# A two-layer streaming encoder step: the first layer's FFN-out as 2x2 blocks in seven products

## The chip, the cores and the metric

The kernel runs on one core of a Trainium2 chip. The metric is the device time of one execution in microseconds, the median of several runs. A core has TensorE (PE in the profile, with its weight loads as PEld), VectorE (DVE), ScalarE (ACT), GpSimd (POOL) and SyncE (SP), which here issues nearly all DMAs. Matmuls take fp32 operands split into two parts of type fp32r, a high and a low one, so a product of two matrices is three passes: high by high, high by low, low by high.

## The reference

One step over 1088 columns (1024 prompt frames and 64 frames of a running stream) with a model width of 1024. Layer 0 has an SSD mixer, layer 1 a chunk-band attention, each followed by a SwiGLU FFN with 2816 hidden rows:

```python
def swiglu(u, w_in, w_out):
    g, up = jnp.split(u @ w_in, 2, axis=-1)
    return (jax.nn.silu(g) * up) @ w_out

# per layer, for the prompt and the sample alike
xp = xp + rmsnorm(mp, nw[1])                      # mp: mixer or attention
xp = xp + rmsnorm(swiglu(rmsnorm(xp, nw[2]), ffn_w_in[layer], ffn_w_out[layer]), nw[3])

# layer 1 starts from the residual stream after layer 0
kv = rmsnorm(x, kv_norm_w) @ w_kv                 # shared K and V
q  = rmsnorm(xp, nw[0]) @ attn_w_q[i]
```

The change touches `... @ w_out` of layer 0, where the sums of weights for both layers are made, and the first weights of `w_kv` and `attn_w_q`.

## The kernel before, in words

Activations lie with features on partitions (tiles of 128 rows) and frames on columns. The work runs in the order SSD mixer, layer 0's FFN-in, layer 0's FFN-out, K/V/Q projections and attention, output projection, layer 1's FFN-in, layer 1's FFN-out.

*The order of the work.* PE's instructions are issued in the order in which the program writes them. A small planner, `Stream` (L94), keeps a simulated time `st.t` that grows by columns/2360 us for each matmul. Side tasks (generators: norm chains, loaders, ends of slices) yield a delay and a condition, and `pump` lets those go on whose time has come, so their few matmuls fall among the main ones at that place in PE's queue. The other engines' instructions are ordered by priority; `tc.high_priority(n)` moves a group ahead. Constants such as `ER_W`, `EQ_W` are such delays. SP issues its DMAs in one queue. `Weights` (L236) holds a list of planned weight tiles: `load` issues the DMA into one of two `raw` buffers (or one lent for the stage), then ACT copies the high part and VectorE subtracts for the low part (`part`, L362 to L372); three such pairs fit. A weight with `kscale` goes through `scaled` (L375): eight ACT and eight VectorE instructions, one per 128 columns, with a norm weight multiplied in.

*FFN-in* of both layers is in seven products (P1 to P7) of 2x2 blocks: rows of the weight by two, frames by two. `BO, BN` split the frames into block 0 (512) and block 1 (576), each of two halves, so matmuls have 256 or 288 columns; the four halves are the quarters q0 to q3 of `QS`. `run_pair` (L1469) does a pair of gate and up tiles, in the order of `RUN[layer]`; its evictions run on ACT and VectorE (`add`, `times`, L1483 to L1535).

*Layer 0's FFN-out* is plain: each of three slices of frames (384, 384, 320), each of 8 blocks of 128 rows, 22 blocks of the hidden dimension, three passes (L1901 to L1903). The hidden activations go to DRAM (`hd`) in FFN-in (class `Plain`, `row`) and come back split by `loader` (L1710). After a slice, `end` (L1792) makes the post-norm, adds the residual from `x1d`, writes `x2d`, splits the result into the operands `u[s]` of attention, and forms the next norm's factor in `rba[s]`; while later slices run, only the last slice's `end` remains beside attention's first units (one unit is a weight tile on a slice: 8 x 3 matmuls).

*Layer 1's FFN-out* is in seven products (`wino`, L1546; matmuls L1596 to L1598). Class `Hidden` forms four sums of blocks of the hidden activation on VectorE in FFN-in (`form`, L1395; the operations are L1408) and stores seven operands in `hop`. The four sums of blocks of the weight (`wt`) are formed in *layer 0's* FFN-in by `Plain.chunk` (L1337, operations on L1347), from loads into the five stage buffers `sg`. Such operations wait in a list `late`; one is issued after each product of `run_pair`. `wino` runs the products in `PHASES`: P1, P6, P2, P7, P5 on both blocks, then P4 on block 0, P4 on 1, P3 on 1, P3 on 0; it keeps P3's weights in SBUF from the first to the second. Quarter q0 is complete after P4 on block 0, q2 after P4 on 1, q3 after P3 on 1, q1 after P3 on 0. `end7` (L1764) ends a quarter.

*Attention's start* (L2221): `wv, wk, wq` of the first pair of heads on slice 0, then on slice 1, then a second `wk` on both, then slice 2. Each evicted unit needs `rba[s]`.

Of the kernel before, what the change touches and what calls it, by code (L numbers as in the profile page):

```python
# [49 lines left out]
ES = 0.5, 0.5, 0.0  # L50
OS = 1.9, 1.4
EP_W, ER_W, EQ_W = (9.4, 9.4, 5.0), (8.9, 8.9, 4.5), (11.0, 11.0, 11.0)
# [5 lines left out]
LDP, ENP, ATP = 1500, (0, 0, 1500), 1000  # L58
# [11 lines left out]
LAHEAD, LGAP = 2, (1.5, 0.5)  # L70
# [3 lines left out]
RUN = (  # L74
    [(t, (0, 1)) for t in range(NB0, FT)] + [(t, (1,)) for t in range(NB0)],
    [(5, (0, 1)), (4, (1,))] + [(t, (0, 1)) for t in range(6, FT)] + [(t, (1,)) for t in range(4)],
)
# [329 lines left out]
PHASES = [(p_, (0, 1)) for p_ in (P1, P6, P2, P7, P5)] + [(P4, (0,)), (P4, (1,)), (P3, (1,)), (P3, (0,))]  # L407
# [4 lines left out]
def hybrid_kernel(  # L412
# [39 lines left out]
    hop = dr.tile([P, 7, KH, T // 2], F32, name="hop")  # L452
    wt = dr.tile([P, 4, 4, FH], F32, name="wt")
# [61 lines left out]
    def add_sq(ssum, src, n, first, eng=None):  # L515
        if first:
            A.activation(ssum[:, :n], src, AF.Square)
        else:
            q = nsb.tile([P, 384], F32, tag="sq", bufs=2, name="sq")
            A.activation(q[:, :n], src, AF.Square)  # L520
            (eng or G).tensor_tensor(ssum[:, :n], ssum[:, :n], q[:, :n], op=ALU.add)  # L521
# [32 lines left out]
    def bcast(dg, a, n, rb=None):  # L554
# [4 lines left out]
        if rb is None:  # L559
            rb = nsb.tile([P, 384], F32, tag="rb", bufs=1, name="rb")  # L560
        A.copy(rb[:, :n], bp[:, :n])
# [703 lines left out]
    def phys(layer, t_):  # L1265
        return t_ // 2 + KH * (t_ % 2) if layer else t_
# [6 lines left out]
    def ffn_plan(layer):  # L1273
        w1, w2 = w_f1[layer], w_f2[layer]
        W.plan(*[dict(src=[w1[i]]) for t_ in range(NB0) for i in (phys(layer, t_), FT + phys(layer, t_))])
        for i, (t_, bs) in enumerate(RUN[layer]):
            it = dict(src=[w1[phys(layer, t_)], w1[FT + phys(layer, t_)]])
# [3 lines left out]
        if not layer:  # L1281
            for s in range(NSL):
                for m in range(KD):
                    for k0, nk in KCH:
                        W.plan(dict(src=[w2[m][:, k0 * P:(k0 + nk) * P]], n=nk * P))
            return
        for p_, _ in PHASES[:-1]:
            for j in range(4):
                for i, (k0, nk) in enumerate(KIT):
                    if p_ in (P1, P2, P3):  # L1290
                        v = half(w2[j + 4 * (p_ == P3)], p_ != P1, k0, nk)
                    else:
                        v = wt[:, j, {P6: WT2, P7: WT3, P5: WT1, P4: WT4}[p_], k0 * P:(k0 + nk) * P]
                    it = dict(src=[v], n=nk * P, lend=1)
                    if p_ == P3 and 2 * j + i >= HLB:
                        it["keep"] = R
                    W.plan(it)

    KCH = ((0, 8), (8, 8), (16, 6))

    class Plain:

        def __init__(self):
            self.late = []

        def order(self, bs):
            pass

        def first(self, b, t_):
            return False  # L1310

        def out(self, b, t_, row, other):
            return other

        def row(self, b, t_, row, v):
            n = v.shape[1]
            nc.sync.dma_start(hd[:, t_, BO[b] + row * n:BO[b] + (row + 1) * n], v)

        def sums(self, b, t_, c, u_):
            pass  # L1320

        def side(self, i):


            if i == 0:
                self.todo, self.got = [(j, k0, nk) for j in range(4) for k0, nk in WCH], []
                self.load()
            if self.todo:
                self.late += [lambda gate, i=i: self.chunk(i, gate) for i in range(4)]

        def load(self):
            w2, (j, k0, nk) = w_f2[1], self.todo[0]
            self.got = [stage[0]()[:, :nk * P] for _ in range(4)]
            for t_, m, h in zip(self.got, (j + 4, j + 4, j, j), (1, 0, 0, 1)):
# [1062 lines left out]
```

## Time and profile before

| | |
|---|---|
| median of 3 runs | 3046.65 us (3046.03 to 3050.11) |
| the profiled execution | 3048.59 us, span of its instructions 3046.8 us |
| mean granted clock of TensorE | 0.988 |
| PE, PEld, DVE, ACT, POOL busy | 97%, 95%, 72%, 48%, 22% of the span |
| DMA | 385.70 MB, 127 GB/s on the mean |
| layer 0: FFN-in; FFN-out | 941 to 1361 us; 1361 to 1635 us of the span |
| layer 1: FFN-in; FFN-out | 2367 to 2791 us; 2791 to 3032 us |

A line of a group reads: line of the kernel, engine, operation, output tile <- input tiles, shape, count | busy us, mean ns of one | idle time of the engine just before them, and what ended it. Matmuls are pipelined, so the mean of one is longer than the distance between two starts; cadences are read from the timeline. In tables by stretch, the columns after the length are the busy us (and instructions) of PE, PEld, DVE, ACT and POOL, then the granted clock, the share of the DMA engines and GB/s.

### The profile page before, as it was taken

What the parts mean: (1) busy time and instruction counts of PE and PEld (TensorE: products, weight loads), DVE (VectorE), ACT (ScalarE), POOL (GpSimd) and SP (SyncE); (2) the same over time, 40 slices, a digit from 0 to 9 for tenths busy, and PEclk for the clock granted to TensorE, in tenths of its full rate; (3) what the DMA queues carried; (4) which work ended last, traced back from release to release, by engine and by line L of the source; (5) the groups of instructions that cost most, each with busy time, mean ns of one, the idle gap of its engine ahead of it and who ended that gap; (6) DMA issues with size and microseconds to landing.
All of it is one profiled execution on the core that took longest, in us unless ns stands there. A gap on an engine that the chain in (4) does not pass through costs nothing. (4 is left out here: it accounts for less than half of the span.)

```text
span 3046.8 us, 58392 instructions
## 1 busy us (share of the span) xinstructions
PE 2949.8 (97%) x22017; PEld 2883.7 (95%) x22017; DVE 2193.8 (72%) x4906; ACT 1475.2 (48%) x2834; POOL 660.6 (22%) x852
## 2 busy tenths in 40 slices
PE   9999999999999999999999999999898999999999
PEld 8899999999999999999999898999898899999998
DVE  8988888885878665684666777767668765558567
ACT  6665656554444333354454655555544433335452
POOL 1334444421342221111231000000053212211011
PEclk9999999999999999999999999999999999999999
DMA  3433333335543544555664222212344333236665
GB/s 119 114 92 103 96 100 96 99 115 164 155 133 118 156 132 152 157 163 171 203 192 135 75 66 81 62 63 73 112 148 132 101 112 119 80 104 201 190 190 190
DMA packets 244843, 385.70 MB, mean 127 GB/s; under 512 B 25584, under 2 KB 197168, under 8 KB 244560
## 3 DMA queue, kind: packets, MB, share of 16 engines
q1 hardware_dynamic: 244496, 381.89, 40.6%
q8 instruction: 173, 2.83, 0.4%
q14 instruction: 110, 0.90, 0.1%
q0 software_dynamic: 64, 0.07, 0.0%
HBM read 293.54 MB, written 83.86 MB: 124 GB/s over the span
## 5 line engine op out<-in xcount | busy, mean ns | idle before, releaser
L495 PE MATMUL mm<-r,hl 128*128 128x384 f32 (+2 forms) x1632 | 548.4, 336 | 7.1 <-ACT r L2210 6.2
L497 PE MATMUL mm<-r,hl 128*128 128x384 f32 (+2 forms) x1632 | 530.2, 325 | 3.5 <-DVE hl L383 2.8
L496 PE MATMUL mm<-r,hl 128*128 128x384 f32 (+2 forms) x1632 | 529.4, 324 | 0.7 <-DVE r L2211 0.7
L371 DVE TENSOR_TENSOR hl<-raw,hl 128x1024 fp32r<-128x1024 f32 (+1 forms) x245 | 287.2, 1174 | 204.4 <-ACT hl L370 203.0
L1501 PE MATMUL px<-r,hl 128*128 128x288 f32 (+1 forms) x1192 | 350.5, 294 | 0.4 <-DVE r L1192 0.3
L370 ACT CAST hl<-raw 128x1024 fp32r<-128x1024 f32 (+1 forms) x245 | 240.8, 984 | 189.8 <-PE po L1903 48.2
L495 PEld LDWEIGHTS mm<-r,hl 128*128 128x128 f32 x1632 | 311.0, 191 | 8.9 <-ACT r L2210 6.4
L1500 PE MATMUL px<-r,hl 128*128 128x288 f32 x1056 | 311.9, 295 | 4.6 <-ACT p L1512 2.6
L497 PEld LDWEIGHTS mm<-r,hl 128*128 128x128 f32 x1632 | 310.2, 190 | 5.0 <-DVE hl L383 4.0
L496 PEld LDWEIGHTS mm<-r,hl 128*128 128x128 f32 x1632 | 311.2, 191 | 1.3 <-DVE r L2211 1.0
L1502 PE MATMUL px<-r,hl 128*128 128x288 f32 x1056 | 311.3, 295 | 0.0
L521 POOL TENSOR_TENSOR ssum<-ssum,sq 128x256 f32<-128x256 f32 (+3 forms) x146 | 157.8, 1083 | 510.0 <-ACT sq L520 494.6
L1500 PE MATMUL px<-rx,hl 128*128 128x256 f32 x816 | 229.7, 281 | 9.9 <-ACT p L1512 9.9
L1502 PE MATMUL px<-rx,hl 128*128 128x256 f32 x816 | 228.5, 280 | 0.0
L1501 PEld LDWEIGHTS px<-r,hl 128*128 128x128 f32 x1192 | 224.3, 188 | 0.9 <-DVE r L1192 0.8
L1500 PEld LDWEIGHTS px<-r,hl 128*128 128x128 f32 x1056 | 199.0, 188 | 6.0 <-ACT p L1512 3.5
L1502 PEld LDWEIGHTS px<-r,hl 128*128 128x128 f32 x1056 | 198.8, 188 | 0.0
L1501 PE MATMUL px<-rx,hl 128*128 128x256 f32 x680 | 190.6, 280 | 0.0
L1489 DVE TENSOR_TENSOR c<-px,u 128x256 f32<-128x256 f32 (+1 forms) x78 | 34.5, 442 | 198.1 <-ACT u L1512 198.1
L1512 ACT COPY u<-px 128x288 f32<-128x288 f32 (+1 forms) x156 | 60.4, 388 | 224.3 <-PE px L1502 224.1
L1500 PEld LDWEIGHTS px<-rx,hl 128*128 128x128 f32 x816 | 155.0, 190 | 10.6 <-ACT p L1512 10.6
L1502 PEld LDWEIGHTS px<-rx,hl 128*128 128x128 f32 x816 | 155.1, 190 | 0.0
(421 smaller groups left out, 8589.8 us busy)
## 6 DMA issues: line engine op xcount, KB each, us to landing
raw<-in_w_f_dram SPq DMA_DIRECT2D x156, 512.0 KB, 3.8
raw<-in_w_in_dram SPq DMA_DIRECT2D x40, 512.0 KB, 3.7
raw<-in_w_so_dram SPq DMA_DIRECT2D x32, 512.0 KB, 3.9
raw<-in_w_f_dram SPq DMA_DIRECT2D x33, 384.0 KB, 3.3
dm<-acd SPq DMA_DIRECT2D x64, 192.0 KB, 3.7
sg<-hop SPq DMA_DIRECT2D x77, 144.0 KB, 3.1
sg<-hop SPq DMA_DIRECT2D x83, 128.0 KB, 3.2
sg<-in_w_f_dram SPq DMA_DIRECT2D x48, 192.0 KB, 3.5
```

What stands on the lines that cost most here:

```text
L370: self.nc.scalar.copy(h, v)
L371: (eng or self.eng or self.nc.vector).tensor_tensor(lo, v, h, op=ALU.subtract)
L495: PE.matmul(ps[:, :n], h_, xh, start=(first and i == 0), stop=False)
L496: PE.matmul(ps[:, :n], h_, xl, start=False, stop=False)
L497: PE.matmul(ps[:, :n], l_, xh, start=False, stop=(last and i == nk - 1))
L521: (eng or G).tensor_tensor(ssum[:, :n], ssum[:, :n], q[:, :n], op=ALU.add)
L1489: V.tensor_tensor(x[d], x[bank][:, :n], x[y or d], op=ALU.add)
L1500: PE.matmul(ps, wh, ah[:, k, :], start=(k == 0 and not on), stop=False, skip_group_check=on)
L1501: PE.matmul(ps, wh, al[:, k, :], start=False, stop=False, skip_group_check=on)
L1502: PE.matmul(ps, wl, ah[:, k, :], start=False, stop=(k == 3), skip_group_check=on)
L1512: A.copy(hid.gate, ps)
```

## The change

Layer 0 uses `Hidden` and `wino` as layer 1 does. `Plain`, `loader`, `end_load` and `end` go. Both layers use layer 1's order of pairs (`RUN`). Each layer has its own `hop` and `wt` in DRAM and forms its weight sums in its own FFN-in, between pairs 2 and 16 (`side`). In layer 0 the last phases are P4 on 0, P4 on 1, P3 on 0, P3 on 1, and P3's weights are loaded for each block. `EndU` ends the quarters of layer 0: attention's slices are cut differently from quarters (`PARTS`), so quarter 1 is split in two parts and quarter 2 gives its last 32 columns to slice 2 in a later step; residuals come through the stage buffers, those of q3 ahead into two `r` buffers. `prescale` multiplies six attention weights by their norm weights during FFN-out and stores them in `wsc` in DRAM; eight planned weights then need no scaling. At attention's start a unit is evicted after the next unit's matmuls.

```diff
-EP_W, ER_W, EQ_W = (9.4, 9.4, 5.0), (8.9, 8.9, 4.5), (11.0, 11.0, 11.0)
+PARTS = [(0, 0, 0, 256)], [(0, 256, 0, 128), (1, 0, 128, 256)], [(1, 128, 0, 256), (2, 0, 256, 288)], [(2, 32, 0, 288)]
+EP_W, ER_W, EQ_W = (3.0, 3.0, 3.0), (5.5, 7.0, 5.5, 4.5), (18.0, 2.5, 14.0, 22.0)
...
+PHASES = [
+    [(p_, (0, 1)) for p_ in (P1, P6, P2, P7, P5)] + end_
+    for end_ in ([(P4, (0,)), (P4, (1,)), (P3, (0,)), (P3, (1,))], [(P4, (0,)), (P4, (1,)), (P3, (1,)), (P3, (0,))])
+]
...
         def order(self, bs):
...
-            for o in g:
-                self.late += o
+            self.late = [f for o in g for f in o] + self.late
...
         def side(self, i):
...
+            if i in (1, 7):
+                self.load()
+            elif self.todo and (i == 2 or 8 <= i < FT - 5):
+                self.late += [lambda gate, i=i: self.chunk(i, gate) for i in range(4)]
+                if i % 2 == 0:
+                    self.late += [lambda gate: None] * 3
+                    self.late += [lambda gate, i=i: self.chunk(i, gate) for i in range(4)]
...
     def wino(...):
...
-                    if p_ != P3:
+                    if p_ != P3 or not layer:
                         W.put()
...
+                if not layer:
+                    if p_ == P4 and j == 0:
+                        W.pri = HIP
+                    if (p_, bs) == phases[-1] and j == 0:
+                        st.spawn(end.ahead())
...
+            def prescale():
+                for i, (v, c) in enumerate(FIRST):
+                    for c0, c1 in ((0, 3), (3, 6), (6, 8)):
+                        t = stage[0]()[:, :(c1 - c0) * P]
+                        nc.sync.dma_start(t, v[:, c0 * P:c1 * P])
+                        yield 0, PS_W
+                        t3 = t.rearrange("p (k m) -> p k m", m=P)
+                        V.tensor_tensor(t3, t3, c[:, c0:c1].unsqueeze(2).to_broadcast([P, c1 - c0, P]), op=ALU.mult)
+                        nc.sync.dma_start(wsc[:, i, c0 * P:c1 * P], t)
+                        yield 0, PS_G
...
+            class EndU:
...
+                def split(self, q, y, m, s, c, c0, c1):
+                    ym = y[m // 4][:, m % 4, c0:c1]
+                    uh, ul = (v[:, c:c + c1 - c0] for v in u[s][m])
+                    with tc.high_priority(ENP[q]):
+                        A.copy(uh, ym)
+                        V.tensor_tensor(ul, ym, uh, op=ALU.subtract)
...
+                def __call__(self, q, y, ss, more):
...
+                    yield from rb_steps(ss, n, out, ER_W[q], more=more)
+                    tot = [ssum_start(n) for _ in range(1 + last)]
+                    def tail(m):
...
+                            self.split(q, y, m, *part)
+                        with tc.high_priority(ENP[q]):
+                            add_sq(tot[m % len(tot)], y[m // 4][:, m % 4, :], n, m < len(tot), G if q < 2 or m % 2 else V, None if last else xs[m])
+                    for m in range(KD):
+                        ym = y[m // 4][:, m % 4, :]
+                        with tc.high_priority(ENP[q]):
+                            V.scalar_tensor_tensor(ym, ym, col(cpost2 + m), out[0], op0=ALU.mult, op1=ALU.mult)
+                            (V if last or m % 2 == 0 else G).tensor_tensor(ym, ym, xs[m], op=ALU.add)
...
+                        if not last:
+                            tail(m)
+                        yield 0, ES[q]
...
+                    yield 0, EQ_W[q]
+                    to = [(rb_out[s][:, c:c + c1 - c0], c0, c1) for s, c, c0, c1 in parts]
+                    yield from rb_steps(tot[0], n, [], ER_W[q], to, more=tot[1] if last else None)
...
+    FIRST = (w_kv[8], kvw), (w_kv[0], kvw), (w_q[0], qw), (w_kv[1], kvw), (w_kv[9], kvw), (w_q[1], qw)
...
-    W.plan(W_V[0], W_K[0], W_Q[0], W_K[1], W_V[0], W_V[1], W_K[1], W_Q[1])
+    W.plan(*[dict(src=[wsc[:, i, :]]) for i in (0, 1, 2, 3, 0, 4, 3, 5)])
...
             for w, e in ((wv, evv), (wk, evk), (wq, evq)):
-                units(w, 0, e, (s,))
+                ps_ = mm("mm")
+                passes(ps_, w, lambda k: u[s][k], [(k, k) for k in range(KD)], SL[s][1], parts=4)
                 if s and w is wv:
                     W.put()
+                open_.append((e(0), s, ps_))
+                if len(open_) > 1:
+                    f, s_, p_ = open_.pop(0)
+                    f(s_, p_)
+                st.pump()
```

More of the change, by code (lines that the diff above doesn't have):

```diff
@@ L1280, in ffn_plan @@
             W.plan(it)
[L1281 to L1287, printed above, removed]
+        for p_, _ in PHASES[layer][:9 - layer]:
             for j in range(4):
```

358 lines of the change are left out of this document (154 added, 204 removed).

## The prediction

> **What bounds the kernel now.** I read the page first, then a table by stage (busy time per engine between two points of the span), the timeline of PE for its cadence, the waits of PE, and last the groups of VectorE's instructions.
>
> ```profile
> span 3046.8 us, 58392 instructions
> PE 2949.8 (97%) x22017; PEld 2883.7 (95%) x22017; DVE 2193.8 (72%) x4906; ACT 1475.2 (48%) x2834; POOL 660.6 (22%) x852
> ```
>
> PE has work in 97% of the span, so a change pays by taking matmuls away or by taking away PE's waits. The stages, in the columns us, PE, PEld, DVE, ACT, POOL, granted clock, DMA share, GB/s:
>
> ```profile
> 941.00:1361.40 420.40, 414.97 (x3284) 414.10 (x3283) 281.76 (x476) 164.40 (x306) 79.50 (x81) 1.00 0.47 145
> 1361.40:1635.00 273.60, 269.95 (x1620) 267.65 (x1619) 153.34 (x223) 126.67 (x217) 54.40 (x46) 0.99 0.60 187
> 2366.60:2791.00 424.40, 414.93 (x3267) 413.29 (x3266) 278.82 (x500) 163.87 (x309) 83.73 (x88) 0.99 0.35 110
> 2791.00:3032.00 241.00, 237.54 (x1886) 235.87 (x1885) 160.09 (x338) 112.91 (x240) 28.41 (x27) 1.00 0.69 203
> ```
>
> These are layer 0's FFN-in and its plain FFN-out, then layer 1's FFN-in and its FFN-out in seven products. The last two rows already show what the first two are to become: the trace holds a model of the changed stage.
>
> **Matmuls removed.** Plain FFN-out issues 8 blocks of rows x 22 x 3 passes on each of three slices: 1056 matmuls of 384 columns and 528 of 320. Seven products issue 7 x 4 x 11 x 3 = 924 on 256 columns (half of block 0) and 924 on 288. The cadence comes from starts of one line a known number of matmuls apart:
>
> ```profile
> 1379.99 0.34 PE L1901 MATMUL po<-r,hl 128*128 128x384 f32 x1
> ...
> 1389.36 0.34 PE L1901 MATMUL po<-rx,hl 128*128 128x384 f32 x1
> ...
> 1603.81 0.31 PE L1902 MATMUL po<-rx,hl 128*128 128x320 f32 x1
> ...
> 1611.71 0.31 PE L1902 MATMUL po<-rx,hl 128*128 128x320 f32 x1
> ...
> 2899.91 0.28 PE L1596 MATMUL po<-r,hl 128*128 128x256 f32 x1
> ...
> 2901.71 0.30 PE L1596 MATMUL po<-r,hl 128*128 128x288 f32 x1
> ...
> 2904.09 0.28 PE L1596 MATMUL po<-r,hl 128*128 128x256 f32 x1
> ```
>
> 54 matmuls in 9.37 us are 0.1735 us each at 384 columns; 54 in 7.90 are 0.1463 at 320; 15 in 1.80 are 0.120 at 256; 18 in 2.38 are 0.132 at 288. Before: 1056 x 0.1735 + 528 x 0.1463 = 260.4 us. After: 924 x (0.120 + 0.132) = 232.8. **Term 1: -27.6 us.** The columns fall by an eighth (574,464 to 502,656), the time by less, because a shorter matmul costs more per column.
>
> **Waits inside the stage.** Before, the stage has 273.6 - 260.4 = 13.2 us beyond its matmuls; layer 1's has 241.0 - 232.8 = 8.2. These are norm matmuls, waits of PE, and what follows a wait: the clock.
>
> ```profile
> PE po L1901 <- ACT hl L370: 2.6, 1, 2.6
> PE nst L528 <- POOL ssum L1833: 4.8, 1, 4.8
> PE mm L497 <- DVE hl L383: 2.8, 2, 2.2
> PE px L1500 <- ACT p L1512: 7.1, 3, 4.4
> PE px L1500 <- ACT p L1512: 5.4, 4, 3.8
> ```
> ```profile
> 1591.20:1598.10 6.90, 6.01 (x21) 5.61 (x22) 5.11 (x5) 4.07 (x8) 3.41 (x4) 0.51 0.55 173
> 1666.30:1673.20 6.90, 6.73 (x25) 6.72 (x25) 4.39 (x17) 1.60 (x4) 0.58 (x4) 0.51 0.43 149
> 1714.10:1717.50 3.40, 3.40 (x12) 3.31 (x13) 2.33 (x8) 1.77 (x6) 0.00 (x0) 0.50 0.11 26
> ```
>
> Right after the 2.6 us wait for a weight (in FFN-out), the 4.8 us wait for a sum of squares (at the handover to attention) and the waits on L383, the clock stands at half for 6.9, 6.9 and 3.4 us, which costs half of that again. In the new stage the last four half-products (P4 on block 0, P4 on block 1, P3 on 0, P3 on 1: 132 x (0.120 + 0.132) x 2 = 66.5 us) each read a weight tile for one block alone, as in layer 1, and layer 0 also reloads P3's weights, which layer 1 keeps. I take 9 us beyond the matmuls, near layer 1's row, with 6 and 13 as bounds. **Term 2: -4 us** (-7 to 0).
>
> **Layer 0's FFN-in** gets layer 1's order of pairs and the hidden sums: 88 tensor-tensors of 256 or 288 columns with as many stores. Their duration is the same shape's in the block below (L1776, 0.415 us): 37 us on a VectorE that is busy for 282 of 420. The order's price is in the waits above: layer 1's three waits for the evicted gate cost 7.1 us, layer 0's four 5.4, and the stages differ by 424.4 - 420.4. **Term 3: +4 us** (0 to +8).
>
> **The 64 weight-sum operations** (L1347, 0.613 us at 384 columns) stand once per FFN-in as before, but now beside the sums in both. In layer 1 that is 278.8 + some 37 = 316 of 424 us, 75%: hidden by VectorE's idle quarter, save that each can make an eviction late by its own length. Without that cover the cost would be its busy time. Their loads and stores go through SP in an FFN-in whose DMA share is 0.35, and the five stage buffers are all taken by one chunk. **Term 4: +2 us** for both stages (0 to +6).
>
> **The handover.** Before, slices 0 and 1 are finished long before attention asks for them; only slice 2's tail is late, and it costs 4.8 us and a half clock of 6.9, together 8.2. After, quarters q0, q2, q1 and q3 finish in the last 51 us, and attention's slice 0 needs q0 and q1, slice 2 needs q3. VectorE has to carry them:
>
> ```profile
> 1560.00:1590.00 30.00, 28.44 (x188) 27.39 (x186) 25.81 (x44) 14.23 (x27) 12.73 (x11) 1.00 0.64 196
> 2962.00:2978.00 16.00, 15.72 (x125) 15.18 (x124) 12.79 (x23) 10.02 (x21) 4.65 (x4) 1.00 0.87 256
> 2978.00:2995.00 17.00, 16.00 (x118) 15.69 (x119) 16.21 (x38) 7.65 (x13) 3.33 (x3) 1.00 0.69 222
> ```
> ```profile
> L371 DVE TENSOR_TENSOR hl<-raw,hl 128x640 fp32r<-128x640 f32 x6 | 4.9, 820 | 2.1 <-ACT hl L370 2.1
> L371 DVE TENSOR_TENSOR hl<-raw,hl 128x768 fp32r<-128x768 f32 x5 | 4.8, 957 | 1.1 <-ACT hl L370 1.0
> L1625 DVE TENSOR_TENSOR u<-po,u 128x288 f32<-128x288 f32 x8 | 3.6, 450 | 0.0
> L1775 DVE SCALAR_TENSOR_TENSOR r<-r,pcs,rb 128x256 f32<-128x256 f32 x4 | 2.3, 613 | 0.0
> L1776 DVE TENSOR_TENSOR r<-r 128x256 f32<-128x256 f32 x4 | 1.5, 415 | 0.0
> L538 DVE TENSOR_TENSOR nv<-nv 128x3 f32<-128x3 f32 x4 | 0.6, 159 | 0.1
> ...
> L1347 DVE TENSOR_TENSOR sg<-sg 128x384 f32<-128x384 f32 x48 | 29.4, 613 | 1.5 <-DVE sg L1341 0.3
> L371 DVE TENSOR_TENSOR hl<-raw,hl 128x1024 fp32r<-128x1024 f32 x180 | 226.0, 1256 | 152.5 <-ACT hl L370 152.4
> L383 DVE SCALAR_TENSOR_TENSOR hl<-raw,pcs,hl 128x128 fp32r<-128x128 f32 x208 | 65.8, 357 | 5.8 <-ACT hl L380 5.6
> ...
> L1828 DVE TENSOR_TENSOR r<-y,r 128x384 fp32r<-128x384 f32 x16 | 15.3, 998 | 1.0 <-ACT r L1827 1.0
> L521 POOL TENSOR_TENSOR ssum<-ssum,sq 128x256 f32<-128x256 f32 x62 | 63.0, 1017 | 246.4 <-ACT sq L520 244.7
> ```
>
> From the end of P4 on block 0 until slice 2's operands stand, VectorE has: three half-products' weights, 12 x (0.957 + 0.820) = 21.3; five attention weights at 1.256 = 6.3; 12 evictions at 0.45 = 5.4; tails of 8 blocks of rows with a scale (0.613), an add and a split (0.415 each), half of the adds on POOL for three quarters: 9.9 + 11.3 + 10.2 + 13.2 = 44.6 with the sums of squares that stay on VectorE; seven norm chains of nine small operations and one 384-column product, 9 x 0.159 + 0.613 = 2.0 each = 14; 14 evictions and splits of attention's first two slices at 0.613 = 8.6. Sum 100 us. PE needs in the same time 132 x (0.132 + 0.120 + 0.132) = 50.7 us and eight units of 24 matmuls at 0.1735 = 33.3, together 84. VectorE is short by 16 us. The row of 1560 to 1590 shows what that does: one slice's tail, VectorE busy for 25.8 of 30 us, and PE idle by 1.6. Some of the 100 us can wait, and SP, ACT and POOL carry their own shares, so I take 12 us of waiting and one half-clock spell of 3.4: 15 in place of 8. **Term 5: +7 us** (-8, if all is hidden, to +53, below). PE's norm matmuls for q1 stand in its queue among attention's first units, and whatever is behind them waits with them.
>
> **The six weights scaled ahead.** Now a scaled weight costs VectorE 8 x 0.357 = 2.9 us, afterwards a plain 1.256, and the 2.8 us waits on L383 with 3.4 us at half clock go. The 18 scalings (0.613 each, 11 us) and their 36 DMAs pass through SP and VectorE between P1 and P5, where layer 1's stage row has VectorE at 160 of 241. **Term 6: -4.5 us** (-4.5 to 0).
>
> Sum: -27.6 - 4 + 4 + 2 + 7 - 4.5 = -23.1. The profiled execution took 3048.6 us, its span and 1.8 us around it, so 3025.5; the median of the runs, 3046.65, is 1.9 below it: **3024 us**, with 3015 to 3033 as its own range.
>
> **Rivals.**
> *The handover costs nothing more* (3009): the slack of slices 0 and 1's 25 us of units covers VectorE's shortage and the 15 us go. For it: q3 is needed last, and casts are halved. Against: 16.2 of 17 us in the row from 2978.
> *Tails stretched by POOL* (3044): the split L1828 took 998 ns beside POOL's sums against 613 for the same shape without them. At 256 columns that is two thirds of 0.385 = 0.26 us on 64 scales and splits, 16 us more: 16 + 16 + 3.4 = 35 in place of 15.
> *DMA sets the pace of the last four half-products* (3030 to 3041). They move weights, 4 x 44 x 64 KB = 11.5 MB; half of P3's operands, 1.5; residuals in, 4.5; results out, 2.2; three attention weights, 1.6: 21.3 MB in 66.5 us, 320 GB/s. The row from 2962 has 256 GB/s at a share of 0.87: at 256 this takes 83 us, at 256/0.87 = 294 it takes 72, so +6 to +17. Against it: buffers loaded ahead. The Trainium skill ("DMA: Bandwidth & Descriptors", Specifications) gives about 358 GB/s for a core from HBM; by that the bytes take 60 us and this rival is nothing. No long stretch here comes near that figure.
> *Slower* (3070): in the same four half-products every scale and split takes as long as POOL's operation, 1.017 in place of 0.415, +0.6 x 64 = 38 us; VectorE is then 54 us short and PE pays that with two half-clock spells, 61 in place of 15. The point from which it decides: 44 us of loss. For it: POOL gets half the adds and most of the sums there. Against: the 998 is a mean for 384 columns where POOL's own operation takes longer than that. The Trainium skill ("SBUF — State Buffer", Who interferes with whom) says that a VectorE instruction with two SBUF inputs blocks fully against a POOL instruction that reads SBUF; by that rule this is the case, and L1828's mean leans its way.
> That the matmuls stay is no rival: their count follows from the loops.
>
> **How the numbers follow.** Forecast 52%, nothing lost at the handover 16%, DMA 10%, stretched tails 13%, slower 9%. What a measurement here can tell from no change is 0.2%, 6.1 us: faster is below 3040.6. The forecast, the first rival, the DMA case and a small part of the stretched tails lie there: 81%; most of the stretched tails lie within: 10%; slower 9%. The range runs from 3009 to 3044: it leaves out the slower case and the outer halves of its neighbours.
>
> **What would show it.** Layer 0's FFN-out should be 242 us (232.8 + 9) with matmuls of 256 and 288 columns, layer 0's FFN-in 425, layer 1's 425. The handover's waits should name VectorE or POOL ahead of attention's first units, on the norm sum or the split. If PE instead waits for weights from DMA in P4 and P3, the DMA rival holds; if the two FFN-ins grow by over 15 us together, terms 3 and 4 are wrong.

## The result and the profile after

| | before | after |
|---|---|---|
| median of 4 runs each, same chip | 3047.55 us | 3063.78 us (3061.74 to 3066.19) |
| ratio, 95% interval | | 1.0053 [1.0035, 1.0070] |
| span of the profiled execution | 3046.8 us | 3063.8 us |

The changed kernel is slower by half a per cent, where 3024 us were forecast and 3044 was the upper end of the range. The page after, its first lines:

```profile
span 3063.8 us, 60130 instructions
...
PE 2934.7 (96%) x22295; PEld 2863.1 (93%) x22295; DVE 2317.7 (76%) x5263; ACT 1476.2 (48%) x2894; POOL 652.6 (21%) x870
```

PE is busy for 15 us less than before (2949.8) and the span is 17 us longer: PE is now idle for 129 us in place of 97. The next table cuts the span by stages and shows where. "Handover" is the time from the last matmul of layer 0's FFN-out to the end of attention's first eight units. Attention's halves are parted at the same matmul of its 42nd unit in every run, and the second ends with the last score matmul.

| us | before | after | difference |
|---|---|---|---|
| layer 0, FFN-in | 419.8 | 432.7 | +12.9 |
| layer 0, FFN-out | 273.3 | 258.2 | -15.0 |
| handover | 45.8 | 60.8 | +15.0 |
| attention, first half | 254.6 | 249.6 | -5.0 |
| attention, second half | 253.6 | 252.8 | -0.8 |
| output projection to FFN-in of layer 1 | 176.6 | 179.0 | +2.4 |
| layer 1, FFN-in | 425.7 | 433.3 | +7.7 |
| layer 1, FFN-out | 240.7 | 240.4 | -0.3 |

The table by stretch (columns as in the prediction) for FFN-in 0, FFN-out 0, handover and FFN-in 1, first of the kernel before, then of the one after:

```profile
941.80:1361.60 419.80, 414.37 (x3278) 413.50 (x3277) 281.16 (x475) 164.40 (x306) 79.39 (x80) 1.00 0.47 146
1361.60:1634.90 273.30, 269.65 (x1617) 267.35 (x1616) 153.04 (x223) 126.57 (x216) 54.40 (x46) 0.99 0.60 187
1634.90:1680.70 45.80, 40.79 (x224) 39.98 (x222) 34.33 (x85) 20.96 (x54) 9.33 (x14) 0.93 0.36 115
2365.50:2791.10 425.60, 416.13 (x3278) 414.49 (x3277) 279.98 (x501) 163.87 (x309) 83.73 (x88) 0.99 0.36 111
```
```profile
941.80:1374.60 432.80, 418.01 (x3279) 415.47 (x3278) 324.55 (x583) 163.53 (x309) 83.48 (x87) 0.99 0.51 163
1374.60:1632.80 258.20, 243.14 (x1881) 239.77 (x1880) 187.47 (x383) 132.70 (x291) 48.25 (x52) 0.98 0.75 228
1632.80:1693.60 60.80, 47.28 (x238) 43.57 (x237) 42.59 (x120) 22.79 (x63) 12.17 (x20) 0.83 0.34 101
2374.90:2808.30 433.40, 416.68 (x3279) 413.86 (x3278) 321.98 (x581) 163.39 (x309) 82.93 (x88) 1.00 0.51 162
```

FFN-out 0 and the handover took 319.1 us together and take 319.0. A rough account of them: idle time of PE (length less busy) was 3.7 + 5.0 = 8.7 us and is 15.1 + 13.5 = 28.6; time lost to the half clock (length times one minus the granted clock, which is printed to a hundredth, so good to 1 or 2 us) was 5.9 and is 15.5. Without both, 304.5 us became 274.9. So the matmuls are saved, 29.6 us, and all of it is given back: 19.9 as idle time and 9.6 as half clock. PE's waits there, from 1532 to 1700 before and from 1540 to 1700 after (engine, line, what for and from whom: us in total, times, longest):

```profile
PE nst L528 <- POOL ssum L1833: 4.8, 1, 4.8
PE po L1901 <- ACT hl L370: 2.6, 1, 2.6
PE po L1903 <- DVE hl L371: 1.1, 2, 0.7
```
```profile
PE nbp L561 <- DVE dg L553: 10.4, 3, 5.5
PE nst L532 <- POOL ssum L525: 5.8, 3, 2.9
PE mm L499 <- DVE r L1793: 5.4, 2, 3.9
PE po L1585 <- DVE hl L370: 2.7, 4, 0.9
```

They stand where the forecast said: at the norm matmuls (`nst`, `nbp`) and at the splits of attention's operands (`r`); 2.7 us are for low parts of weights. None is for a weight from DMA. Most of the last three half-products (1559.8 to 1632.8), and the time after:

```profile
1574.00:1592.00 18.00, 14.70 (x105) 14.29 (x104) 16.11 (x27) 10.31 (x25) 11.07 (x13) 0.91 0.70 214
1592.00:1612.00 20.00, 17.85 (x142) 17.32 (x141) 19.86 (x38) 10.84 (x23) 9.78 (x11) 1.00 0.69 210
1612.00:1633.00 21.00, 14.91 (x88) 13.93 (x87) 18.86 (x50) 10.27 (x25) 9.42 (x10) 0.84 0.75 227
1633.00:1660.00 27.00, 17.57 (x71) 14.80 (x70) 17.86 (x62) 6.74 (x23) 8.49 (x11) 0.68 0.29 90
```

VectorE is busy for 54.8 of 59 us up to 1633. In the 27 us behind that, with waits of 3.9 and 2.9 us among them, the granted clock is 0.68.

The first five products took 166.1 us for their 1320 matmuls; at the forecast's cadences they are 166.3. What FFN-out 0 takes beyond its matmuls therefore lies in the last four half-products: 92.2 us (from 1540.7) against 66.5, with VectorE busy for 82.2. Layer 1's four, the forecast's model, took 74.6 in the kernel before (2957.3 to 3031.9), with VectorE busy for 60.4. The stretch for which the forecast set 100 us of VectorE against 84 of PE, from the end of P4 on block 0 to the end of the eight units:

```profile
1559.80:1693.60 133.80, 108.21 (x665) 102.30 (x664) 108.37 (x257) 61.44 (x147) 46.22 (x56) 0.88 0.55 165
```

VectorE's 108.4 us are near the 100. But PE is idle for 25.6 us, and 133.8 x 0.12 = 16 us are lost to the clock.

### The profile page after: what moved, and what is told of

Its sections match the earlier page's. It is cut to its first block, busy times and chain, and to the rows that moved or that the text cites. A ratio compares the mean times of both kernels' runs of the same rounds, so it can differ in the third digit from the quotient of the medians.

```text
span 3063.8 us, 60130 instructions
## 1 busy us (share of the span) xinstructions
PE 2934.7 (96%) x22295; PEld 2863.1 (93%) x22295; DVE 2317.7 (76%) x5263; ACT 1476.2 (48%) x2894; POOL 652.6 (21%) x870
## 5 line engine op out<-in xcount | busy, mean ns | idle before, releaser
L370 DVE TENSOR_TENSOR hl<-raw,hl 128x1024 fp32r<-128x1024 f32 (+2 forms) x230 | 257.1, 1119 | 120.6 <-ACT hl L369 119.0
L498 PEld LDWEIGHTS mm<-r,hl 128*128 128x128 f32 x1632 | 312.7, 192 | 11.5 <-ACT r L2195 6.0
L369 ACT CAST hl<-raw 128x1024 fp32r<-128x1024 f32 (+2 forms) x230 | 216.8, 943 | 135.5 <-PE po L1585 44.1
L525 POOL TENSOR_TENSOR ssum<-ssum,sq 128x288 f32<-128x288 f32 (+1 forms) x142 | 147.3, 1039 | 434.5 <-ACT sq L524 412.6
L1583 PE MATMUL po<-rx,hl 128*128 128x256 f32 (+1 forms) x650 | 189.3, 291 | 1.7 <-ACT p L1606 1.7
L1585 PE MATMUL po<-rx,hl 128*128 128x256 f32 (+1 forms) x650 | 188.6, 290 | 2.5 <-DVE hl L370 2.5
L1584 PE MATMUL po<-rx,hl 128*128 128x256 f32 (+1 forms) x650 | 188.0, 289 | 0.0
L1485 PEld LDWEIGHTS px<-rx,hl 128*128 128x128 f32 x816 | 155.2, 190 | 20.3 <-ACT p L1497 20.3
```

What stands on the lines that cost most here:

```text
L369: self.nc.scalar.copy(h, v)
L370: (eng or self.eng or self.nc.vector).tensor_tensor(lo, v, h, op=ALU.subtract)
L498: PE.matmul(ps[:, :n], h_, xh, start=(first and i == 0), stop=False)
L1485: PE.matmul(ps, wh, ah[:, k, :], start=(k == 0 and not on), stop=False, skip_group_check=on)
L1583: PE.matmul(ps[b][:, :n], wh, xh, start=(k == 0), stop=False)
L1584: PE.matmul(ps[b][:, :n], wh, xl, start=False, stop=False)
```

## The experiments

Two questions: what makes both FFN-ins longer (20.6 us), and what eats the matmuls' gain at the end of FFN-out 0 (24.5 us against the forecast). A single execution counts for little as a total: ten of one of these kernels ran from 3043.7 to 3055.0 us. The verdicts therefore go by stages, and by intervals where there are some. FFN-out 0 and handover together scatter too: e3 and e15, one program, have 314.2 and 317.9 us; e1 and e2, which differ there from the changed kernel only in the weights that they load, 323.1 and 322.7 beside its 319.0. Differences of some 4 us in that sum are called within the scatter below.

### The two FFN-ins

**e1: no weight sums.** The sums, their loads and their stores are left out; layer 0's and layer 1's P6, P7, P5 and P4 take a plain quarter of the weight in place of a sum, so these products are other ones. (The line that takes the plain quarter is not shown, here and in e2.)

```diff
-            if i in (1, 7):
-                self.load()
-            elif self.todo and (i == 2 or 8 <= i < FT - 5):
+            if self.todo and 0 and (i == 2 or 8 <= i < FT - 5):
```

> Leaves out the forming of the weight sums of both layers (its loads, operations and stores); the four products that need them read a block of the raw weight instead, same bytes, so the output is not the reference's. In the changed kernel layer 0's FFN-in takes 432.7 us and layer 1's 433.3, against 419.8 and 425.7 before. Theory A (the weight sums, made now beside the hidden sums, hold VectorE up on DMAs): both FFN-ins fall to about 425 (layer 1's of before, which had hidden sums alone), and the execution by some 15 us, to about 3049. Rival B (the hidden sums and layer 1's order of pairs cost layer 0 its part): layer 1's falls to 425, layer 0's stays near 432. Rival C (the two new FFN-ins are slow by the DMA traffic of the sums alone): as A here; the next run tells.

**e2: sums without their stores.** Loads and operations stay, only the stores to `wt` are left out; the same products take a plain quarter.

```diff
             V.tensor_tensor(o_, x_, y_, op=op)
-            nc.sync.dma_start(self.wt[:, j, i_, k0 * P:(k0 + nk) * P], o_)
```

> Leaves out only the 128 stores of the weight sums; loads and operations stay, and the products read a block of the raw weight. VectorE's work is that of the changed kernel. Theory A (VectorE stands behind the stores and loads of a chunk that reuses the five stage buffers at once): the waits of the chunk's first operation on its store, 18.4 us in layer 0, go, and both FFN-ins fall by 5 us or more, to 428 or less. Rival D (VectorE's 40 us more of work in each FFN-in is the cost, through late evictions): both stay at 431 to 433.

**e3: three empty places ahead of the first chunk as well.** Nothing is left out; in a step that issues two chunks, three products pass before the first one's four operations, as they do before the second's.

```diff
+                if i % 2 == 0 and i > 2:
+                    self.late += [lambda gate: None] * 3
                 self.late += [lambda gate, i=i: self.chunk(i, gate) for i in range(4)]
```

> Computes what the changed kernel does; three empty places are put also ahead of the first of two chunks that follow each other, so that no chunk stands right behind another. Theory A: VectorE's waits on stores and loads of chunks fall from 25 us in layer 0 to under 12, and each FFN-in by 3 to 6 us; the execution to about 3056. Rival D (work, not waits): no change, 3062 to 3065.

Measured: 3052.65, 3052.59 and 3043.48 us beside 3047.32 for the kernel before. FFN-in 0 took 425.3, 425.7 and 427.1 us (432.7 after), FFN-in 1 424.2, 426.1 and 426.2 (433.3). FFN-in 0's row of e1, then of e2, then of e3:

```profile
941.50:1366.80 425.30, 416.00 (x3279) 415.17 (x3278) 282.57 (x503) 163.85 (x309) 83.08 (x87) 0.99 0.35 112
```
```profile
941.80:1367.50 425.70, 416.35 (x3278) 415.16 (x3277) 324.03 (x583) 162.33 (x309) 84.17 (x87) 0.99 0.44 139
```
```profile
942.20:1369.30 427.10, 416.05 (x3278) 415.10 (x3277) 321.89 (x583) 163.39 (x309) 82.95 (x87) 0.99 0.52 165
```

Between e1 and e2 VectorE has 41 us more work, and the stage is 0.4 us longer (1.9 in layer 1): the sums' operations cost next to nothing, and the rival that put the cost on them (D) falls. Between e2 and the changed kernel there are only the stores, and the two stages are 7.0 and 7.2 us longer, as theory A said. e3, with all the stores and 165 GB/s, shows that it isn't the traffic. VectorE's waits between 1000 and 1375 in the changed kernel, and in e3, where L1408 is the same line as L1406:

```profile
DVE sg L1406 <- DMA wt<-sg: 18.4, 8, 3.7
...
DVE sg L1412 <- DMA sg<-in_w_f_dram: 7.1, 7, 2.1
```
```profile
DVE sg L1414 <- DMA sg<-in_w_f_dram: 6.2, 7, 1.9
...
DVE sg L1408 <- DMA wt<-sg: 1.9, 2, 1.1
```

The chunk's first operation writes a stage buffer whose content of the chunk before is still on its way to DRAM. VectorE stands at it for up to 3.7 us, and behind it in VectorE's order stand the evictions that PE's next product waits for (PE idle in FFN-in 1: 433.4 - 416.7 = 16.7 us, in e2 9.5). In the changed kernel's trace six waits of PE over 0.5 us in FFN-in 0 (5.3 us together) and seven in FFN-in 1 (6.9) come within 13 us of the end of such a wait of VectorE; e2 has none of them. Three products in between give the store time to land. In e3's one execution the handover was 4 us shorter too, with the same waits; the timed run below did not repeat that.

**e15: e3 timed in rounds.**

> The kernel with the three empty places again, timed in rounds: 3043 to 3045 beside a kernel before of 3045 to 3047, a ratio of 0.998 to 1.0005. If its one look of 3043.5 was luck of the half-clock spells (10 us of spells fewer than the changed kernel between 1580 and 1750, 5 us of time), 3044 to 3049.

Measured: 3048.35 us (10 runs) beside 3043.42 (13), ratio 1.0014 [1.0004, 1.0025]. Its FFN-ins again took 425.7 and 425.8 us; FFN-out 0 and handover took 317.9 in place of 314.2, at a clock of 0.84 in place of 0.88 in the handover. So the empty places take back the FFN-ins' part of the loss, and e3's further gain did not come back. That is the expectation's second case, luck of the half-clock spells.

### The end of FFN-out 0 and the handover

All of these but e4 have the three empty places, so that e3 and e15 are what they stand beside. "Lost" is length times one minus the clock, as above.

| us | FFN-out 0 | handover | sum | PE idle | lost | VectorE busy | GpSimd busy |
|---|---|---|---|---|---|---|---|
| before | 273.3 | 45.8 | 319.1 | 8.7 | 5.9 | 187.4 | 63.7 |
| after | 258.2 | 60.8 | 319.0 | 28.6 | 15.5 | 230.1 | 60.4 |
| e3 | 257.4 | 56.8 | 314.2 | 27.0 | 14.5 | 230.8 | 60.5 |
| e15 | 258.0 | 59.9 | 317.9 | 26.8 | 17.3 | 230.3 | 61.1 |
| e4 P3 first | 256.6 | 53.2 | 309.8 | 21.2 | 12.0 | 230.7 | 62.8 |
| e5 no low parts | 245.9 | 61.5 | 307.4 | 19.2 | 13.5 | 203.4 | 54.2 |
| e6 broadcast later | 246.6 | 66.3 | 312.9 | 27.4 | 9.9 | 228.3 | 61.8 |
| e7 P3 first | 257.2 | 53.3 | 310.5 | 24.6 | 9.4 | 232.3 | 63.1 |
| e9 P3 first, no low parts | 249.4 | 50.9 | 300.3 | 18.5 | 5.5 | 202.6 | 56.5 |
| e10 no GpSimd in tails | 255.2 | 48.7 | 303.9 | 18.0 | 8.5 | 214.6 | 29.4 |
| e11 P4 on both | 240.0 | 82.0 | 322.0 | 31.6 | 24.5 | 221.1 | 61.2 |
| e12 tails on VectorE | 262.6 | 45.0 | 307.6 | 24.8 | 10.1 | 227.7 | 32.6 |
| e13 e12 and P3 first | 253.8 | 57.7 | 311.5 | 29.4 | 11.4 | 229.0 | 37.0 |
| e14 adds only, P3 first | 259.5 | 47.8 | 307.3 | 24.6 | 6.6 | 229.8 | 51.5 |
| e16 e12 again | 263.0 | 44.8 | 307.8 | 24.7 | 10.1 | 227.7 | 32.1 |
| e17 e12, q2's sum later | 247.4 | 60.5 | 307.9 | 21.1 | 10.9 | 226.4 | 32.4 |

**e4: P3 on block 0 ahead of P4 on block 1** (on the changed kernel; with it, q1's first part is split at once and its second in a later step).

```diff
-    for end_ in ([(P4, (0,)), (P4, (1,)), (P3, (0,)), (P3, (1,))], [(P4, (0,)), (P4, (1,)), (P3, (1,)), (P3, (0,))])
+    for end_ in ([(P4, (0,)), (P3, (0,)), (P4, (1,)), (P3, (1,))], [(P4, (0,)), (P4, (1,)), (P3, (1,)), (P3, (0,))])
```

> Computes what the changed kernel does; layer 0's last four half-products run as P4 on block 0, P3 on block 0, P4 on block 1, P3 on block 1, so that quarters 0 and 1, which attention's first units need, are complete 35 us before the end and not 17 us. The changed kernel takes 92.1 us for the four, against 66.4 of matmuls, and 60.8 us from there to the end of attention's first eight units, against 45.8 before. Theory E (quarter 1's tail is late): the wait of attention's first units for its split, 5.4 us, and the half clock of 17 us behind it go; four half-products and handover together fall from 153 to about 140, the execution to about 3050. Rival F (VectorE's total work over the last four half-products and the handover sets the end): the two together stay within 4 us of 153, with other waits in other places.

Measured: 3055.47 us; the handover fell to 53.2 us, FFN-out 0 stayed, and their sum fell by 9.2 us of the 13 of theory E. Attention's first slice needs q0 and q1, which now end first.

**e5: no low part for the last half-products' weights** (their third matmul takes the high part again, so these products are other ones).

```diff
+            if 'thin' in it:
+                lo = h
+            else:
                 (eng or self.eng or self.nc.vector).tensor_tensor(lo, v, h, op=ALU.subtract)
```

> Edit, on top of the three empty places of the run before: in layer 0's last four half-products the low part of each weight is not computed; the matmul of the low part takes the high part again (so these products miss the weight's low part). VectorE loses 32 subtractions of 0.8 to 1.4 us, some 30 us of the 104 that it is busy between 1540 and 1660; PE's instructions are the same. Theory F (the end of layer 0's FFN-out and the first units of attention are short of VectorE): the two segments together, 314 us in the run with the empty places, fall by 15 to 30, time 3013 to 3028. Theory Q (PE stands in its queue behind the norm matmuls of the quarters, which are issued too early for VectorE's chain of small operations): those waits are shorter by what the chain was interrupted, -3 to -10, and the rest stays.

**e9: e5 and the order of e4.**

> Edit: the three empty places, no low part for the weights of layer 0's last four half-products (their third matmul takes the high part again), and P3 on block 0 ahead of P4 on block 1. Two causes are supposed for the 24 us lost between layer 0's FFN-out and attention's first eight units: VectorE too slow for the last four half-products (11 us, which the run without low parts gave back inside FFN-out) and a late quarter q1, which attention's first slice needs (8 us, which the other order gave back in the handover). If they are two, the segments are 246 and 53 us and the time 3027 to 3032. If VectorE's shortage is one debt that any order only moves (without low parts FFN-out lost 11 us and the handover got 5 of them back), the sum of both segments stays at 305 to 310 as in each of the two alone, time 3038 to 3044.

Measured: e5 3038.64 us, e9 3029.85. In e5 VectorE has 27 us less to do; FFN-out 0 fell by 11.5 us, but the handover, whose chains are q1's and q3's, did not. The sum fell by 6.8 (e3) or 10.5 us (e15): theory Q's 3 to 10, not the 15 to 30 of theory F, which takes VectorE's busy time for the whole cause. With both, the sum is 300.3 and the time in the band forecast for two causes: the gains add up within the scatter.

**e6: the norm's broadcast later in PE's queue.**

```diff
-EP_W, ER_W, EQ_W = (3.0, 3.0, 3.0), (5.5, 7.0, 5.5, 4.5), (18.0, 2.5, 14.0, 22.0)
+EP_W, ER_W, EQ_W = (3.0, 3.0, 3.0), (11.0, 12.5, 11.0, 4.5), (18.0, 2.5, 14.0, 22.0)
```

> Edit, on top of the three empty places: the time between a quarter's norm sum and its broadcast on PE is 11, 12.5 and 11 in place of 5.5, 7 and 5.5 us of matmuls for quarters 0, 1 and 2. Nothing is left out. Theory Q: the waits on the broadcast (1.6 and 5.5 us before 1620) go and with them a half-clock spell of 6.8, -6 to -12 us: 3032 to 3038. Theory F: VectorE is busy for 93% of that stretch and its work is the same, so the waits move to the evictions and to attention's operands: within 3 us of 3043, or later tails make it slower, up to 3050.

Measured: 3046.13 us. FFN-out 0 is 10.8 us shorter than in e3 and the handover 9.5 longer. The waits moved, as theory F said; theory Q's 6 to 12 us did not come.

**e7: e3 with the order of e4.**

> Edit: the three empty places, and P3 on block 0 ahead of P4 on block 1. If the two gains are of different places (20 us and 8 us alone, of which the first has 14 from the FFN-ins and 5 from the handover), they add up to 3063 - 14 - 9 = 3040 or, if the empty places' 5 us in the handover stay too, 3035. If the order helps only because it gives VectorE time, as the empty places' gain in the handover may, 3042.

Measured: 3048.41 us, a miss as a total. The handover is e4's 53 us again; attention's first half, 253.4 us in place of e3's 246.9, with 15 us at half clock where e3 had none, took it back. That the total is 5 us above e3's one execution is within the scatter of e15.

**e10: no GpSimd in the tails.** Its residual adds and its additions of squares are left out (the code cut shows the adds alone).

```diff
-                            (V if last or m % 2 == 0 else G).tensor_tensor(ym, ym, xs[m], op=ALU.add)
+                            if last or m % 2 == 0:
+                                V.tensor_tensor(ym, ym, xs[m], op=ALU.add)
```

> Edit, on top of the three empty places: in the quarters' tails of layer 0 GpSimd does nothing: its adds of the residual (every second block of quarters 0, 1 and 2) and its additions of squares are left out (the squares themselves are still made on ScalarE), so the outputs lack them. VectorE's instructions are the same but for none added. If VectorE's scales and splits are stretched by GpSimd, theory P (0.7 to 0.95 us beside GpSimd's operations, 0.41 alone): FFN-out and handover together, 314 us with the empty places, fall by 8 to 16, time 3028 to 3036. If the stretch is small against the number of operations: 310 to 314, and only the waits on GpSimd's norm sum go (2.4 and 2.9), 3038 to 3042.

Measured: 3032.23 us. GpSimd is busy for 31 us less, and VectorE, with the same instructions, for 16.2 us less (230.8 to 214.6); the sum of both segments falls by 10.3 (14.0 against e15), as theory P forecast. Groups of VectorE in the last 87 us of FFN-out 0 in the changed kernel, then in the last 84 of e10, where L1795 and L1842 are the lines L1793 and L1835:

```profile
L1793 DVE TENSOR_TENSOR r<-r 128x256 fp32r<-128x256 f32 x4 | 3.2, 790 | 0.0
...
L1835 DVE SCALAR_TENSOR_TENSOR u<-u,pcs,rb 128x288 f32<-128x288 f32 x4 | 2.9, 744 | 0.0
L1793 DVE TENSOR_TENSOR r<-u,r 128x256 fp32r<-128x256 f32 x4 | 2.7, 702 | 0.0
```
```profile
L1842 DVE SCALAR_TENSOR_TENSOR u<-u,pcs,rb 128x288 f32<-128x288 f32 x4 | 2.0, 509 | 0.0
...
L1795 DVE TENSOR_TENSOR r<-r 128x256 fp32r<-128x256 f32 x4 | 1.7, 414 | 0.0
L1795 DVE TENSOR_TENSOR r<-u,r 128x256 fp32r<-128x256 f32 x4 | 1.6, 412 | 0.0
```

Not every group became shorter: the splits `r<-c,r` of 128x256 took 430 ns on the mean in the changed kernel and 550 in e10. What e10 shows is the sum.

**e11: P4 on both blocks in one phase.**

```diff
-    for end_ in ([(P4, (0,)), (P4, (1,)), (P3, (0,)), (P3, (1,))], [(P4, (0,)), (P4, (1,)), (P3, (1,)), (P3, (0,))])
+    for end_ in ([(P4, (0, 1)), (P3, (0,)), (P3, (1,))], [(P4, (0,)), (P4, (1,)), (P3, (1,)), (P3, (0,))])
```

> Edit, on top of the three empty places: layer 0's P4 runs on both blocks in one phase, like the five ahead of it, so that its eight weights are loaded and split once in place of twice. Nothing is left out. VectorE has 8 subtractions of 0.8 to 1.0 us less, 7.6, and the four quarters' tails start later: q0 and q2 together after P4. If VectorE's total decides (theory F), FFN-out and handover together fall by 4 to 8 from 314, time 3036 to 3040. If it is the order in which the quarters' chains come (theory E), q0's tail now stands 16 us later beside q2's and the sum grows by 5 to 15, 3048 to 3058.

Measured: 3052.03 us, as theory E said. With the tails out of its way FFN-out 0 takes 240.0 us, as layer 1's does (240.4). The tails then all fall behind it: 82 us of handover, with one wait of 16.6 us for GpSimd's norm sum.

**e12: the tails' GpSimd work on VectorE**, with nothing left out, and **e13: that with the order of e4**.

```diff
-                            add_sq(tot[m % len(tot)], y[m // 4][:, m % 4, :], n, m < len(tot), G if q < 2 or m % 2 else V, None if last else xs[m])
+                            add_sq(tot[m % len(tot)], y[m // 4][:, m % 4, :], n, m < len(tot), V, None if last else xs[m])
...
-                            (V if last or m % 2 == 0 else G).tensor_tensor(ym, ym, xs[m], op=ALU.add)
+                            V.tensor_tensor(ym, ym, xs[m], op=ALU.add)
```

> Edit, on top of the three empty places: GpSimd's residual adds and its additions of squares in the quarters' tails stand on VectorE; nothing is left out. With the same work left out altogether the two segments fell from 314 to 304 and VectorE's busy time in them by 16 us. Now VectorE gets 12 adds and some 20 additions of 0.42 to 0.45 back, 14 us. If GpSimd's cost is the stretch of VectorE's operations (theory P, stretch): 16 off and 14 on, the sum stays at 312 to 316, time 3042 to 3046. If it is that the norm sums come late from GpSimd, whose additions take 1.0 us (theory P, late): the waits on GpSimd's sum go (5.3 us and the half clock behind them), 306 to 310, time 3034 to 3040.

> Edit: as the run before, with P3 on block 0 ahead of P4 on block 1. If the order's gain (4 to 9 us in the two segments) and GpSimd's are independent: the sum is 4 to 6 below that of the run before. If both give VectorE's chains the same time, they are equal within 3.

Measured: 3035.26 and 3041.60 us. In e12 VectorE takes over some 30 instructions and is busy for 3.1 us less than in e3, as 16 off and 14 on would have it. But the sum of segments falls to 307.6, where the stretch of VectorE's operations alone would have left it at 312 to 316: this is the band of norm sums that come late from GpSimd. The waits of PE on these sums did not simply go, though; in FFN-out 0 one of 12.9 us on VectorE's sum stands in their place (shown under e17). With the other order (e13) the sum is 311.5, against a forecast of a lower or an equal one, so the order's gain did not come on top; 3.9 us are within the scatter.

**e14: only the adds on VectorE, order of e4.**

> Edit: the three empty places, P3 on block 0 ahead of P4 on block 1, and only the 12 residual adds moved from GpSimd to VectorE; the additions of squares stay on GpSimd. Stretch alone: 12 adds of 0.42 on VectorE, +5, against a third of the 16 us of stretch, -5: the two segments stay at 310. If a late scale-and-add chain decides (a block's split waits for GpSimd's add of 1 us in place of 0.42): 305 to 308.

Measured: 3042.85 us, sum 307.3, in the band of the late chain, but only 3 us below e7: within the scatter, so it decides nothing.

**e16: e12 timed; e17: e12 with q2's second norm sum later** (`EQ_W[2]` 30 in place of 14).

> The three empty places and all of the quarters' tails on VectorE, timed in rounds. Its one look was 3035.3 beside a kernel before of 3043.4, and the kernel with the empty places alone spread over 3043.7 to 3055 in ten runs, so a single look can be 5 us off: if the gain on the empty places alone (7 us in the two segments, 314 or 318 to 307.6) holds, 3036 to 3042 and a ratio to before of 0.996 to 0.999. If it was luck of the half-clock spells, 1.000 to 1.002.

> Edit, on top of the run beside it: quarter 2's second norm sum (the one that the second slice's outputs are divided by) goes to PE 30 in place of 14 us of matmuls after its tail. In the profile of the run without this PE stood at it from 1615.7 to 1628.6, 12.9 us, while VectorE worked on quarter 1's tail without a pause. Theory Q (PE's place in the queue): the last matmuls of FFN-out run in that time, attention's first units begin ahead, -5 to -10 us. Theory F (VectorE's work): PE then waits for quarter 1's splits in place of the sum, which are ready at 1628 in either case, 0 to -4 us.

Measured: 3038.64 us (10 runs) and 3039.16 (9 runs) beside 3046.81; ratios 0.9974 [0.9965, 0.9984] and 0.9975 [0.9964, 0.9985]. PE's longest waits between 1540 and 1700 in e16, then in e17:

```profile
PE nst L532 <- DVE ssum L525: 12.9, 1, 12.9
PE nbp L561 <- DVE dg L553: 6.3, 3, 2.8
PE mm L498 <- DVE vt L2048: 2.0, 2, 1.1
```
```profile
PE nbp L561 <- DVE dg L553: 6.7, 3, 2.8
PE nst L532 <- DVE ssum L525: 3.1, 1, 3.1
PE mm L498 <- DVE vt L2048: 3.0, 2, 1.7
PE mm L499 <- DVE r L1795: 2.9, 3, 1.3
PE mm L498 <- ACT r L1794: 2.2, 3, 1.4
```

The wait of 12.9 us shrinks to 3.1, FFN-out 0 falls by 15.6 us, and the handover grows by 15.7: 307.8 and 307.9. Theory F's -4 to 0 came, theory Q's -10 to -5 did not: PE only stands elsewhere until VectorE is through with q1's tail.

### The weights scaled ahead

**e8: e3 with the six weights scaled as they come, as before the change.**

The call that starts `prescale` is left out too.

```diff
-    W.plan(*[dict(src=[wsc[:, i, :]]) for i in (0, 1, 2, 3, 0, 4, 3, 5)])
+    W.plan(W_V[0], W_K[0], W_Q[0], W_K[1], W_V[0], W_V[1], W_K[1], W_Q[1])
```

> Edit, on top of the three empty places: the six attention weights are no longer scaled ahead; each is scaled as it comes, in eight pieces on ScalarE and VectorE, as before the change. Term 6 of the forecast has 4.5 us for this: attention's first half was 254.6 before and is 246.9 with the empty places. If that segment's gain is the scaling ahead: 252 to 255 here, time 3047 to 3050, and with VectorE short in the handover another 2 to 6 us more, since each scaled weight costs it 2.9 in place of 1.3 us. If the gain has another cause: 247 and 3043.

Measured: 3055.84 us. Attention's first half takes 251.7 us in place of 246.9 (e3) and 247.5 (e15), the handover 61.0 in place of 56.8 and 59.9, FFN-out 0 255.4 in place of 257.4 and 258.0. Between 1630 and 1945 this kernel has a wait that e3 has not:

```profile
PE mm L500 <- DVE hl L382: 18.4, 4, 8.8
```

So scaling ahead is worth 4.2 to 4.8 us in attention. What it gains in the handover (1 to 4 us) it costs in FFN-out 0 (2.0 to 2.6), as far as the scatter lets one see: the sum of both is 316.4, between e3 and e15.

## Why the prediction was wrong

The steps gave -23.1 us, the span grew by 17.0. Of the 40 us between them the FFN-ins hold 14.6, FFN-out 0 with the handover 24.5, and the rest is small.

*Term 1, the matmuls (-27.6): right.* The first five products took 166.1 us where its cadences give 166.3, and the account above has 29.6 us less of work at full clock.

*Term 3, layer 1's order and the hidden sums (+4): right.* Without the weight sums FFN-in 0 is 5.5 us longer than before, with them but without their stores 5.9, inside its 0 to +8.

*Term 4, 64 weight sums (+2): the step that failed was its price for the buffers.* The operations cost 0.4 and 1.9 us, as forecast. The forecast also said that one chunk takes all five stage buffers, and then priced only evictions that are late by an operation's length. What a chunk meets is the store of the chunk before: VectorE stands for up to 3.7 us at a time, and that costs 7.0 and 7.2 us of the stages. The forecast's own mark, over 15 us for both FFN-ins together, was passed with 20.6.

*Term 2, waits inside FFN-out 0 (9 us beyond the matmuls, 6 to 13 as bounds): mis-sized.* It measured 258.2 - 232.8 = 25.4 us, all of it in the last four half-products. Its bounds came from layer 1's stage, where VectorE is busy for 60.4 of the 74.6 us of the last four; with layer 0's tails beside them it is busy for 82.2 of 92.2. Without the weights' low parts (e5), or with the tails behind FFN-out 0 (e11), the term is 13 and 7.

*Term 5, the handover (+7, as 15 us in place of 8): the waits came where the forecast put them; the step that failed is the sum that sized them.* It set 100 us of VectorE against 84 of PE, short by 16, and made of that 12 us of waiting and 3.4 us for one half-clock spell. VectorE was busy for 108.4 us in that stretch, near the count, but PE was idle for 25.6 us (some of it in term 2's stage) and lost 16 to the clock, of which the handover alone 60.8 x 0.17 = 10.3. The shortage of busy time alone does not set the wait: e5 takes 27 us from VectorE, more than the shortage, and gets 6.8 to 10.5 back; e12 leaves VectorE's busy time within 3 us and gets 6.6 to 10.3 back. That chains of small operations, which alternate between engines, set it instead fits e10, e11 and e17, but no run takes such a chain apart.

*The rival with tails stretched by GpSimd (3044, 13%)* had the size of the stretch right: 16 us more on VectorE's scales and splits, 16.2 measured in e10. That the stretch was the largest cause is not shown: the sum of e12 speaks for sums that come late from GpSimd as well. By the Trainium skill ("SBUF — State Buffer", Who interferes with whom) a VectorE instruction with two SBUF inputs contends with a GpSimd instruction that reads SBUF; here 31 us less of GpSimd's busy time gave VectorE 16 us, half of it, which agrees. *The slower rival (3070)* asked for every scale and split to take as long as GpSimd's operation, 38 us in all; that did not happen. It set these two segments 46 us above the forecast. They came out 24.5 above, and the time came near its 3070 only with the FFN-ins' 14.6 us, which are no part of it. *The handover at no cost (3009)* and *DMA (3030 to 3041)* fell: no wait of PE is for a weight's DMA, and the DMA share in the last half-products is 0.69 to 0.75.

*Term 6, the scaled weights (-4.5): right*, 5.0 us in attention's first half, and e8 gives 4.2 to 4.8 back.

It stays open how the 24.5 us divide among the weights' splits, the order and GpSimd. The single gains (7 to 10, 4 to 9, 10 to 14 us) come to 21 to 33; those of e5 and e4 add up in e9, those of e12 and e4 do not in e13.

## What to carry to other kernels

Where an operation reuses a buffer that is being stored, its price is the landing of that store for all that stands behind it on its engine: leave a few steps between. Two lines brought 14 us back in the FFN-ins. At the end of a stage follow the chains and don't rely on sums of busy time, count a part of GpSimd's time as VectorE's, and see a moved wait as paid only if the sum of both stretches falls. Together the empty places and the tails on VectorE make the change pay, by a quarter of a per cent: 0.9974 of the time before.

## What was not expected of the hardware

More work on the busiest helper made the kernel faster: in e12 VectorE took over all of GpSimd's adds in the tails and was still busy for 3.1 us less. And the half clock turned small differences into microseconds: e3 and e15 are the same program with nearly the same waits at the handover (12.4 and 12.8 us of idle time), and their granted clock was 0.88 and 0.84 there, which is 3 us of the difference of their totals.
